# Three Gram groups take turns with two pmv groups, in place of following them

## The chip, the cores and the metric

The kernel runs on one core of one Trainium2 chip. The metric is device time in microseconds, as the median of several runs. One execution was also recorded by the hardware profiler; its rows are quoted below. TensorE (PE in the rows, its weight loads PEld), VectorE (DVE), ScalarE (ACT), GpSimd (POOL) and SyncE (SP) are the five engines.

## The reference

One inference step of a two-layer model for 512 latent and 128 context tokens of width 2048, in float32. Layer 0 holds two kinds of attention heads. Layer 1, in which the change lies, is a bidirectional RWKV-7 mixer with 32 heads of 64 channels. After projections that give r, k, v, a gate and, per direction, a decay w and a rate a, it runs this scan over the tokens, once forwards and once backwards:

```python
def step(s, inp):
    r_t, w_t, k_t, v_t, kk_t, a_t = inp
    sa = jnp.einsum('bhij,bhj->bhi', s, -kk_t)
    s = s * w_t[:, :, None, :] + sa[..., None] * (kk_t * a_t)[:, :, None, :] + v_t[..., None] * k_t[:, :, None, :]
    return s, jnp.einsum('bhij,bhj->bhi', s, r_t)
```

The two directions are normalised per head, get a bonus term (the sum over a head of r, k and a weight, times v), are added, gated and projected.

## The kernel before, in words

**Units.** Layer 1 works on 16 tiles of 128 channels (two heads h). Each tile has two units, u = 0 and u = 1, so that `seq` (line 1443) lists 32 units. A unit covers one order of the two directions z over ten chunks of 64 tokens, five per half of the tokens. Instead of stepping through tokens, a unit builds small matrices per chunk and carries the state S over five steps.

**Stages of a unit**, as far as they matter here, each a generator that yields where other work may come between:

- `stage_e` (lines 1077 to 1114) builds AR and BK, the decayed factors, on VectorE. BK has one buffer only. For each half of the tokens VectorE runs L1093, L1096, L1104, L1108 and L1109 one behind the other; L1109 is the last to write BK. AR (L1097, L1100) has two buffers.
- `stage_a2` (1116 to 1133) forms the Gram matrices GG = BK' AR, in three groups of 4, 4 and 2 chunks. A group has 16, 16 or 8 matmuls (L1126) into two PSUM banks at once, one per head; VectorE empties both with a mask (L1130).
- `stage_bk` transposes BK in three groups (L1200), and ScalarE stores the result as BKn (L1201).
- `stage_pre` (1213 ff.) first transposes v in two groups (pvt, L1220; ScalarE writes UV, L1223), then multiplies GG with UV in two pmv groups of 32 and 8 matmuls (L1236), one bank each; ScalarE stores them as MV (L1238). MV is read by the next unit's scan (L1330).
- `stage_inv` inverts small blocks in four steps. `stage_bonus` (1410 ff., only for u = 0) makes two pbn matmul pairs (L1021), each followed by a product on VectorE that writes vT (L1417).
- `stage_c` is the scan itself, five steps with three yields each.

gram, pbk, pvt, pmv, pbn and a few others all take their banks from one PSUM pool, `pg`, with two banks. A tile gets whichever bank is free first.

**The order.** TensorE's order is written out by hand (`manual_schedule`, line 1547 ff.); the planner leaves it alone and orders the other engines itself, by the order in which the code emits instructions, some of it lifted by `high_priority`. `unit(n)` (line 1483) emits first the scan of unit n with other stages at its yields, then `stage_e` of unit n + 2, and then goes through the list `P2` (line 1477): each entry takes one step of a stage, `inv`, `bk` and `pre` of unit n + 1, `a2` of unit n + 2, `bonus` of unit n, and then `fill(w)` inserts projection matmuls (L126, two per step) in proportion to the weight w. The projections of r, k, v and the gate are the bulk of TensorE's work and are spread over all units as filler; where a gate projection ends, ScalarE and VectorE work on the tile `gt` (L947, L952, L957). The weights of `P2` add up to 32.

In the old list the two pvt steps come early (`pre` in the fifth and tenth entry), the second half of the bonus in the eleventh, then both pmv groups, then the three Gram groups. The prologue before the first unit has a script of its own, which the change leaves as it is. Units 0 to 29 have both chains.

Of the kernel before, what the change touches and what calls it, by code (L numbers as in the profile page):

```python
# [53 lines left out]
def kernel(  # L54
# [785 lines left out]
    with ExitStack() as l1:  # L840
# [609 lines left out]
        def of(stage, n):  # L1450
            return stage(*seq[n]) if n < len(seq) else iter(())
# [22 lines left out]
                next(work[0], None)  # L1474

        CW = (3, 3, 2, 3)
        P2 = (('inv', 1), ('bk', 2), ('inv', 2), ('bk', 1), ('pre', 2), ('inv', 2), ('bonus', 1), ('bk', 1), ('inv', 2), ('pre', 2), ('bonus', 2), ('pre', 2), ('pre', 2), ('a2', 3), ('a2', 3), ('a2', 4))
        W2 = sum(w for _, w in P2)

        def step(g):  # L1480
            next(g, None)

        def unit(n):
# [25 lines left out]
            gens = dict(inv=inv, bk=of(stage_bk, n + 1), a2=of(stage_a2, n + 2), pre=of(stage_pre, n + 1), bonus=bonus)  # L1509
            for k, w in P2:  # L1510
                step(gens[k])
# [173 lines left out]
```

## Time and profile before

| what | us |
|---|---|
| median of 3 runs (3610.61 to 3622.48) | 3617.58 |
| the profiled execution | 3616.01 |
| its span, from the first to the last instruction | 3614.2 |
| TensorE busy in it | 3429.2 |
| VectorE busy in it | 2121.4 |

Layer 1's units lie between about 1640 and 3370 us of the span. In a row of the timeline the first number is the start in us, the second the duration, then the engine, the line, the operation, what it writes and reads, shapes and a count; in brackets stands how long the engine was idle before it and what ended that. In a row of the groups the numbers behind the bar are busy time, the mean duration of one in ns, and the idle time before them with those who ended it. In the table of windows they are length, busy time with the count, the granted clock as a share of the full one, and the share and rate of DMA.

### The profile page before, as it was taken

What the parts mean: (1) busy time and instruction counts of PE and PEld (TensorE: products, weight loads), DVE (VectorE), ACT (ScalarE), POOL (GpSimd) and SP (SyncE); (2) the same over time, 40 slices, a digit from 0 to 9 for tenths busy, and PEclk for the clock granted to TensorE, in tenths of its full rate; (3) what the DMA queues carried; (4) which work ended last, traced back from release to release, by engine and by line L of the source; (5) the groups of instructions that cost most, each with busy time, mean ns of one, the idle gap of its engine ahead of it and who ended that gap; (6) DMA issues with size and microseconds to landing.
All of it is one profiled execution on the core that took longest, in us unless ns stands there. A gap on an engine that the chain in (4) does not pass through costs nothing. (4 is left out here: it accounts for less than half of the span.)

```text
span 3614.2 us, 84002 instructions
## 1 busy us (share of the span) xinstructions
PE 3429.2 (95%) x34432; PEld 3004.6 (83%) x34432; DVE 2121.4 (59%) x4218; ACT 1564.7 (43%) x3214; POOL 1217.8 (34%) x1158
## 2 busy tenths in 40 slices
PE   8999999999999989899999999999999999999998
PEld 4788889988898888898887878788888888888898
DVE  3355655666666494536665666666676666666302
ACT  3244443444444422444544534444445445544322
POOL 1322222222232344543333333333333333333444
PEclk9999999999999999999999999999999999999999
DMA  9623433333333365332232222222222222233434
GB/s 324 228 73 99 126 100 111 109 108 108 108 105 107 114 222 166 107 97 66 70 75 60 73 63 69 72 66 68 72 71 70 72 68 72 70 77 104 153 98 143
DMA packets 388610, 376.23 MB, mean 104 GB/s; under 512 B 200512, under 2 KB 242560, under 8 KB 388224
## 3 DMA queue, kind: packets, MB, share of 16 engines
q1 hardware_dynamic: 388224, 370.86, 34.9%
q8 instruction: 270, 4.42, 0.5%
q14 instruction: 116, 0.95, 0.1%
HBM read 328.51 MB, written 42.24 MB: 103 GB/s over the span
## 5 line engine op out<-in xcount | busy, mean ns | idle before, releaser
L101 POOL TENSOR_TENSOR wlo<-raw,whi 128x512 fp32r<-128x512 f32 (+1 forms) x628 | 863.8, 1376 | 1917.9 <-PE pj L126 1207.8
L126 PE MATMUL pj<-h0hi,wlo 128*128 128x320 f32 x4448 | 1087.0, 323 | 25.3 <-POOL wlo L101 25.2
L126 PE MATMUL pj<-h0hi,whi 128*128 128x320 f32 x4448 | 1083.2, 322 | 4.3 <-ACT whi L100 3.1
L126 PE MATMUL pj<-h0lo,whi 128*128 128x320 f32 x4448 | 1077.1, 321 | 2.9 <-DVE h0lo L101 1.6
L126 PEld LDWEIGHTS pj<-h0hi,wlo 128*128 128x128 f32 x4448 | 746.2, 191 | 60.8 <-POOL wlo L101 30.0
L126 PEld LDWEIGHTS pj<-h0hi,whi 128*128 128x128 f32 x4448 | 744.3, 191 | 37.7 <-issue 7.7
L126 PEld LDWEIGHTS pj<-h0lo,whi 128*128 128x128 f32 x4448 | 747.4, 190 | 31.3 <-issue 8.0
L100 ACT ACTIVATE whi<-raw 128x512 fp32r<-128x512 f32 (+1 forms) x628 | 390.8, 623 | 752.5 <-PE pj L126 385.6
L200 DVE SCALAR_TENSOR_TENSOR aacc<-araw,scs,aacc 128x512 f32<-128x512 f32 x480 | 408.5, 900 | 17.4 <-DMA araw<-in_dram 16.3
L364 DVE TENSOR_REDUCE nm<-S 128x1 f32<-128x768 f32 (+1 forms) x120 | 98.5, 820 | 258.3 <-PE S L376 258.3
L1340 ACT ACTIVATE UV<-CC 64x128 f32<-64x128 f32 x160 | 43.2, 270 | 336.6 <-PE CC L1338 307.9
L724 DVE SCALAR_TENSOR_TENSOR x<-pj,mod,xr 128x512 f32<-128x512 f32 (+2 forms) x68 | 33.3, 526 | 250.9 <-PE pj L126 245.3
L367 ACT ACTIVATE P<-S,nm 128x768 f32<-128x768 f32 (+1 forms) x120 | 95.2, 793 | 165.7 <-DVE nm L364 165.0
L1130 DVE TENSOR_TENSOR GG<-gram,con 128x512 f32<-128x512 f32 (+1 forms) x192 | 107.5, 596 | 75.7 <-PE gram L1126 75.4
L1126 PE MATMUL gram<-AR,BK 64*128 64x128 f32 x1280 | 116.6, 296 | 19.3 <-DVE GG L1130 12.3
L1126 PEld LDWEIGHTS gram<-AR,BK 64*128 64x128 f32 x1280 | 92.5, 192 | 44.8 <-DVE GG L1130 23.3
L1062 PE MATMUL plo<-lr,lw 96*128 96x320 f32 x256 | 103.4, 486 | 9.8 <-DMA lr<-lorad 7.3
L566 PE MATMUL po<-PT,vt 128*128 128x128 f32 x800 | 103.2, 276 | 0.1
L566 PEld LDWEIGHTS po<-PT,vt 128*128 128x128 f32 x800 | 98.0, 191 | 4.2 <-issue 2.5
L1354 DVE TENSOR_TENSOR S<-CC,S 128x128 f32<-128x128 f32 (+1 forms) x112 | 29.9, 267 | 119.4 <-PE CC L1305 79.8
L1330 DVE SCALAR_TENSOR_TENSOR rhs<-CC,MV 128x128 f32<-128x128 f32 x160 | 46.2, 289 | 71.1 <-PE CC L1328 70.8
L1338 PEld LDWEIGHTS CC<-rhs,xd 64*64 64x64 f32 x1280 | 50.0, 134 | 41.9 <-DVE rhs L1330 19.5
(340 smaller groups left out, 5164.3 us busy)
## 6 DMA issues: line engine op xcount, KB each, us to landing
raw<-in_dram SPq DMA_DIRECT2D x612, 256.0 KB
araw<-in_dram SPq DMA_DIRECT2D x384, 256.0 KB
lr<-lorad SPq DMA_DIRECT2D x128, 120.0 KB
Ld<-GG SPq DMA_DIRECT2D x64, 160.0 KB
lw<-in_dram SPq DMA_DIRECT2D x128, 48.0 KB
x<-in_dram SPq DMA_DIRECT2D x16, 320.0 KB
xr<-in_dram SPq DMA_DIRECT2D x16, 320.0 KB
DD<-Xd SPq DMA_DIRECT2D x32, 160.0 KB
```

The lines of the kernel that those rows point to most:

```text
L100: act.activation(out=hi, in_=src, func=AF.Copy)
L101: (lo_eng or pool).tensor_tensor(out=lo, in0=src, in1=rf(hi), op=ALU.subtract)
L126: pe.matmul(p[:n, 0:b - a], w, x[:, kk ^ flip, a:b], start=(kk == order[0] and i == 0), stop=(kk == order[-1] + kc - 1 and i == 2))
L200: dve.scalar_tensor_tensor(out=acc[:, s], in0=raw, scalar=scs[:, k, s:s + 1], in1=acc[:, s], op0=ALU.mult, op1=ALU.add)
L364: dve.tensor_reduce(out=nm, in_=S[:, 0:nk], axis=AX.X, op=ALU.max, negate=True)
L367: act.activation(out=P[:, 0:nk], in_=S[:, 0:nk], func=AF.Exp, bias=nm, accum_out=l)
L566: pe.matmul(po[:, 0:128], H.vt[:, kt, :], PT[:, j, :], start=(j == 0), stop=(j == n - 1))
L1062: pe.matmul(ps[:, 0:HT], lw, lo, start=True, stop=True)
L1126: pe.matmul(ps[:, j * 128:(j + 1) * 128], BK[hs, c + j, :, :].rearrange("p a t -> p (a t)"), AR[hs, c + j, :, :].rearrange("p a t -> p (a ...
L1130: dve.tensor_tensor(out=GG[:, c:c + n, h, :], in0=ps[:, 0:n * 128].rearrange("p (j t) -> p j t", t=128), in1=maskg.rearrange("p (o t) -> p ...
L1330: dve.scalar_tensor_tensor(out=rhs.rearrange("p (h d) -> p h d", h=2), in0=C, scalar=-1.0, in1=un.MV[:, s, :].rearrange("p (h d) -> p h d" ...
L1338: pe.matmul(pu[z][o:o + 64, hs], xd[o:o + 64, 2 * loc[z] + h, :], rhs[o:o + 64, hs], start=True, stop=True)
```

## The change

In the second half of the list the Gram steps move between the pmv steps: pmv, pmv, Gram, Gram, Gram becomes Gram, pmv, Gram, pmv, Gram. The weight behind the first two Gram steps goes from 3 to 2 and that behind the pmv steps from 2 to 3; the last keeps 4, and the sum stays 32.

```diff
         CW = (3, 3, 2, 3)
-        P2 = (('inv', 1), ('bk', 2), ('inv', 2), ('bk', 1), ('pre', 2), ('inv', 2), ('bonus', 1), ('bk', 1), ('inv', 2), ('pre', 2), ('bonus', 2), ('pre', 2), ('pre', 2), ('a2', 3), ('a2', 3), ('a2', 4))
+        P2 = (('inv', 1), ('bk', 2), ('inv', 2), ('bk', 1), ('pre', 2), ('inv', 2), ('bonus', 1), ('bk', 1), ('inv', 2), ('pre', 2),
+              ('bonus', 2), ('a2', 2), ('pre', 3), ('a2', 2), ('pre', 3), ('a2', 4))
         W2 = sum(w for _, w in P2)
```

## The prediction

> **What bounds the kernel now.** I read first the page's head and busy times, then the groups of instructions, then the timeline of the part of a unit that the change rearranges, and last the table of windows with the granted clock.
>
> ```profile
> span 3614.2 us, 84002 instructions
> PE 3429.2 (95%) x34432; PEld 3004.6 (83%) x34432; DVE 2121.4 (59%) x4218; ACT 1564.7 (43%) x3214; POOL 1217.8 (34%) x1158
> L1126 PE MATMUL gram<-AR,BK 64*128 64x128 f32 x1280 | 116.6, 296 | 19.3 <-DVE GG L1130 12.3 <-ACT MV L1238 5.4 <-DVE BK L1109 0.4
> L1236 PE MATMUL pmv<-UV,GG 64*64 64x64 f32 x1280 | 51.1, 223 | 1.9 <-ACT MV L1238 1.6
> ```
>
> TensorE is busy for 95% of the span and its order is written out by hand, so what the change can move is the time in which TensorE stands still in front of its next instruction; the amount of its work stays. The last two rows give that time for the two chains that are to alternate: 19.3 us before the Gram matmuls and 1.9 us before the pmv matmuls, 21.2 us together. That is 0.6% of the span, and with it the ceiling for the direct gain of a better order. Of it 12.3 us is TensorE waiting for VectorE to empty Gram's PSUM banks into GG, and 7.0 us (5.4 and 1.6) for ScalarE to empty pmv's into MV.
>
> Next comes the tail of unit 6 (u = 0), from the last transpose of BK to the second Gram group.
>
> ```profile
> 2020.77 0.38 PE L1200 MATMUL pbk<-con,BK 128*128 128x128 f32 x2
> 2021.19 0.90 DVE L1093 TENSOR_TENSOR BK<-kk,az 128x320 f32<-128x320 f32 x2 [0.31 <-PE pbk L1200]
> 2022.00 1.56 DVE L1096 TENSOR_TENSOR BK<-BK,rate 128x320 f32<-128x320 f32 x2
> 2023.48 0.79 DVE L1104 TENSOR_SCALAR az<-az,vecs,ck 128x320 f32<-128x320 f32 x2
> 2024.09 0.46 PE L1021 MATMUL pbn<-hl,blkr 128*128 128x320 f32 x2
> 2024.19 0.88 DVE L1108 TENSOR_TENSOR az<-kT,az 128x320 f32<-128x320 f32 x2
> 2025.00 0.88 DVE L1109 TENSOR_TENSOR BK<-az,rate 128x320 f32<-128x320 f32 x2
> 2025.35 1.15 PE L1236 MATMUL pmv<-UV,GG 64*64 64x64 f32 x32
> 2025.80 0.48 DVE L1417 TENSOR_TENSOR vT<-vT,pbn 128x320 f32<-128x320 f32 x1
> 2027.50 0.45 PE L1236 MATMUL pmv<-UV,GG 64*64 64x64 f32 x8
> 2028.95 1.16 PE L1126 MATMUL gram<-AR,BK 64*128 64x128 f32 x16
> 2030.73 1.28 DVE L1130 TENSOR_TENSOR GG<-gram,con 128x512 f32<-128x512 f32 x2
> 2031.46 1.75 PE L1126 MATMUL gram<-AR,BK 64*128 64x128 f32 x16
> ```
>
> What is to be seen here decides the case. BK has one buffer. The next unit's BK cannot be written before the last transpose (L1200, 2020.77) has read the old one, and then VectorE needs five pairs of instructions, one behind the other (L1093, L1096, L1104, L1108, L1109), before the first half of BK is whole at 2025.00 + 0.44 = 2025.44. The first pmv group starts at 2025.35, in the same tenth of a microsecond. The first Gram group, which reads that BK, comes only at 2028.95, so today it has 3.5 us to spare. The two pmv groups and the projection matmuls behind them are its cover.
>
> **The change part by part.** *Work.* It adds and removes no instruction. Three Gram groups (16, 16 and 8 matmuls) and two pmv groups (32 and 8) stay, the sum of weights stays 32, so each unit gets as many projection steps as before. No step that issues a DMA moves: the store of GG follows the third Gram group, which keeps its place with its weight of 4. So nothing changes on SP's and POOL's queues, and the cost of the work is nothing.
>
> *The first Gram group moves to the place of the first pmv group.* It will now stand at the time at which the trace has that pmv group start; call it T. Two things must be done by then. The first half of BK (end of the first L1109) is one. The other is PSUM: the pool has two banks and a Gram group takes both at once, where a pmv group takes one. In units with u = 0 the bank used before is that of the second pbn matmuls, and it is free when the second L1417 has read it, in unit 6 at 2025.80 + 0.48 = 2026.28, that is 0.93 us after T. That a pmv group could go round this bank is seen in unit 10:
>
> ```profile
> 2247.66 1.15 PE L1236 MATMUL pmv<-UV,GG 64*64 64x64 f32 x32
> 2250.03 0.73 DVE L1109 TENSOR_TENSOR BK<-az,rate 128x320 f32<-128x320 f32 x1
> 2250.58 0.45 PE L1236 MATMUL pmv<-UV,GG 64*64 64x64 f32 x8 [0.70 <-ACT MV L1238]
> 2250.93 0.50 DVE L1109 TENSOR_TENSOR BK<-az,rate 128x320 f32<-128x320 f32 x1
> 2251.35 0.47 DVE L1417 TENSOR_TENSOR vT<-vT,pbn 128x320 f32<-128x320 f32 x1
> ```
>
> The second pmv group started at 2250.58 behind MV, before L1417 had even begun: it took the bank that the first pmv group had left. The Gram group cannot, and would stand from 2247.66 to 2251.82, 4.2 us. I read the same off the thirty units that have both chains: T from the first pmv group, and the later of the first L1109's end and, for u = 0, the second L1417's end. The first and the last of the thirty:
>
> ```profile
> 1697.84 0.88 DVE L1109 TENSOR_TENSOR BK<-az,rate 128x320 f32<-128x320 f32 x2
> 1698.19 1.15 PE L1236 MATMUL pmv<-UV,GG 64*64 64x64 f32 x32
> 1698.64 0.48 DVE L1417 TENSOR_TENSOR vT<-vT,pbn 128x320 f32<-128x320 f32 x1
> ...
> 3268.73 1.15 PE L1236 MATMUL pmv<-UV,GG 64*64 64x64 f32 x32
> L1109 DVE TENSOR_TENSOR BK<-az,rate x1: 933/933/933, 3270.2 to 3270.2; 128x320 f32<-128x320 f32 x1
> ```
>
> They give 1698.64 + 0.48 - 1698.19 = 0.93 us and 3270.21 + 0.93 - 3268.73 = 2.41 us. The fifteen units with u = 0 add up to 25.2 us, the fifteen with u = 1 to 16.3, together 41.5. One unit has none; in the quiet ones it is 0.5 to 0.9 us, the bare length of VectorE's row of instructions; where VectorE also has the gate projection's gt in between it is 1.2 to 4.2. TensorE takes its instructions in order, so the projection matmuls behind the Gram group wait too, and since TensorE is the full engine nothing gives that time back. Term: **+41.5 us**. From below, if only the bare row of instructions remained, thirty times 0.85 or 25 us; nothing only if VectorE's order changed.
>
> *The waits that go.* Behind the change each evacuation has another chain's group and five units of weight before its bank is asked for again by its own chain. The 7.0 us behind MV should go, and the wait of the second and third Gram group for GG. But the first pmv group now comes two units of weight behind the first Gram group and needs a bank of it. Two units lasted 2026.50 to 2027.50, 1.0 us; three, between Gram groups, 2030.11 to 2031.46, 1.35 us. The first of the two GG evacuations needs 0.64 us of its own, so it fits, unless VectorE is late, as it was here, 0.6 us behind the end of the group. I leave half of the 12.3 us standing (6.1), and the 0.4 us for BK, which is in the prologue. Term: 21.2 - 6.1 - 0.4 = **-14.7 us**; the bounds are 0 and -21.
>
> *The clock.* A wait costs more than its length when it halves TensorE's granted clock.
>
> ```profile
> 1918.62 2.67 PE L1126 MATMUL gram<-AR,BK 64*128 64x128 f32 x16 [2.60 <-DVE GG L1130]
> 1918.82:1925.64 6.82, 6.82 (x35) 0.50 0.27 79
> 2147.51:2150.92 3.41, 3.41 (x16) 0.50 0.45 96
> 2195.30:2198.71 3.41, 3.41 (x20) 0.50 0.23 71
> 3277.33:3284.15 6.82, 6.38 (x31) 0.50 0.64 234
> 2386.44:2389.86 3.42, 3.42 (x39) 1.00 0.29 76
> 1915.41:1918.82 3.41, 0.81 (x6) 1.00 0.11 27
> 2191.89:2195.30 3.41, 2.11 (x20) 1.00 0.00 2
> 2249.91:2253.32 3.41, 2.74 (x31) 1.00 0.35 112
> ```
>
> The columns are length, TensorE's busy time and count, clock, DMA. Four stretches at 0.50 lie in or just behind these tails, 20.46 us in all, and half of each is lost: x35 in 6.82 us against x39 in 3.42 at full clock. They follow stretches of 3.41 us in which TensorE was busy for 0.81 and 2.11 us; one with 2.74 was not followed by any. If the waits that cause them go, that is 20.46 / 2 = **-10.2 us**. The new waits bring others. Eight of the thirty are 1.8 us or longer, more than the 1.3 us that the stretch with 2.11 lacked, so I let each of the eight halve the clock for the mean of those seen, 20.46 / 4 = 5.1 us, and lose 2.6: **+20.5 us**, with bounds of 0 and, were all 29 waits to do it, 8 x 2.6 + 21 x 1.7 = 56.
>
> Here a rule speaks otherwise. The Trainium skill, "TensorE: Matmul & The Clock Gate", section "HAM oscillation — how this bites in real kernels", puts the abstract rule as "no PE-idle gaps >~3.4µs". By it only the wait of 4.2 us could halve the clock, and the sum would lack nearly all of the last term. The row with 2.11 us busy disagrees: 1.3 us of idle time was enough. I keep the trace's price and carry the rule's outcome as a rival.
>
> *Sum.* 41.5 - 14.7 - 10.2 + 20.5 = +37.1 us. The profiled execution took 3616.0 us (its span of 3614.2 and 1.8 around it), which gives 3653.1; the median of the runs, 3617.6, lies 1.6 above it, so I predict **3655 us**, 1.0% slower.
>
> **The rivals.** *No new halvings* (0.20). The waits come as forecast but are spread so that no stretch lacks enough. For it: the row with 0.7 us idle (2.74 busy) kept its clock. Against: the one with 1.3 us did not. Sum 41.5 - 14.7 - 10.2 = +16.6, 3634 us.
>
> *Only the bare row of VectorE instructions remains* (0.12). The order on VectorE is the planner's and not written out, and it may put gt's instructions behind BK's when the Gram group is next. Then 25 - 14.7 - 10.2 = 0, 3618 us: nothing to see.
>
> *The cover outlasts the move: faster* (0.10). If the planner puts L1417 and L1109 ahead of gt and of the second halves, BK and the bank are ready at T, as in the one unit without a wait. Then only the gains are left, -14.7 - 10.2 = -24.9, 3593 us. It decides from the point at which the waits at the first Gram group fall below 24.9 us in all, 0.83 a unit. Against it: after the last transpose the five pairs have VectorE to themselves in the quiet units, and still end 0.1 us (u = 0) to 0.8 us (u = 1) behind T, with L1417 behind them.
>
> *Every wait halves the clock* (0.08): 41.5 - 14.7 - 10.2 + 56 = +73, 3690 us.
>
> That the change does not do what it says is no case: the list is the order in which the kernel writes TensorE's groups, and the planner leaves that order as written.
>
> **How the numbers follow.** The forecast has 0.50; its own range, with 25 to 41.5 us of waits and 15 to 35 for the clock, is 3635 to 3675. What a measurement of this kernel can tell from no change is about 0.3%, 11 us, so up to 3628 counts as no change. Slower: forecast, first and last rival, 0.78; same 0.12; faster 0.10. The range from 3613 to 3685 leaves out the faster case and most of the last.
>
> **What would show it.** In the changed kernel the idle time before the Gram matmuls should be 35 to 45 us, most of it in front of first groups, released by BK (L1109) for u = 1 and by vT (L1417) for u = 0; that before the pmv matmuls under 8 us; idle time behind MV near zero; and eight or so stretches at half clock right behind first Gram groups between 1690 and 3290 us. If first Gram groups start at T without idle time, the forecast is wrong by its largest term; if they wait and the clock holds, by its last.

## The result, and the profile after

The changed kernel takes 3656.5 us (median of 4 runs, 3646.2 to 3659.8) against 3615.0 us for the old one (median of 4, one more than when the forecast was made): a ratio of 1.0114, 95% interval 1.0085 to 1.0142. It is slower by 41.5 us, 1.1%; 37 were forecast, over the median known then. The profiled execution took 3653.6 us. Its head, and the groups of the two chains:

```profile
span 3651.8 us, 84032 instructions
PE 3431.3 (94%) x34432; PEld 3006.2 (82%) x34432; DVE 2123.0 (58%) x4218; ACT 1572.0 (43%) x3214; POOL 1207.6 (33%) x1158
L1126 PE MATMUL gram<-AR,BK 64*128 64x128 f32 x1280 | 110.4, 296 | 36.3 <-DVE BK L1109 28.4 <-DVE vT L1417 5.0 <-ACT pj L109 1.1
L1236 PE MATMUL pmv<-UV,GG 64*64 64x64 f32 x1280 | 54.8, 233 | 22.5 <-DVE GG L1130 22.3
```

TensorE's busy time is the same to 2 us of 3430, and the span is 37.6 us longer. The idle time before the two chains rose from 19.3 + 1.9 = 21.2 us to 36.3 + 22.5 = 58.8 us, which is 37.6 us as well. That the two figures agree to the tenth is chance: the busy time grew by 2.1 us, and TensorE's other idle time fell by 2.1. Who is waited for has changed: before it was GG and MV in front of Gram, now it is BK and vT in front of Gram, and GG in front of pmv.

The same tail of unit 6 on the timeline of the changed kernel, with VectorE's rows and those of the two chains:

```profile
2032.03 0.89 DVE L1093 TENSOR_TENSOR BK<-kk,az 128x320 f32<-128x320 f32 x2 [0.31 <-PE pbk L1200]
...
2035.84 0.88 DVE L1109 TENSOR_TENSOR BK<-az,rate 128x320 f32<-128x320 f32 x2
2036.46 0.46 PE L1126 MATMUL gram<-AR,BK 64*128 64x128 f32 x2 [0.20 <-ACT gt L947]
2036.64 0.48 DVE L1417 TENSOR_TENSOR vT<-vT,pbn 128x320 f32<-128x320 f32 x1
2037.17 1.16 PE L1126 MATMUL gram<-AR,BK 64*128 64x128 f32 x14 [0.25 <-DVE vT L1417]
...
2037.50 0.80 DVE L1389 TENSOR_REDUCE gst<-ysq 128x10 f32<-128x640 f32 x1
2038.22 0.54 DVE L952 SCALAR_TENSOR_TENSOR gt<-pj,vecs,gt 128x320 f32<-128x320 f32 x1
2038.68 1.27 DVE L1130 TENSOR_TENSOR GG<-gram,con 128x512 f32<-128x512 f32 x2
2039.41 1.15 PE L1236 MATMUL pmv<-UV,GG 64*64 64x64 f32 x32
```

From L1093 to the end of the first L1109 it takes 4.3 us, as before. The Gram group starts 0.18 us behind that end, at 2036.46; the row puts its wait of 0.20 us down to ScalarE's gt (L947) and not to BK, which was ready at 2036.28. It is stopped after two of its sixteen matmuls, and goes on when L1417 has emptied the second bank. So these rows show the second half of the forecast's mechanism, the bank. The first half, the wait for BK, stands clearly in a unit with u = 1 that is shown below (3089.24, 0.89 us).

### The profile page after: what moved, and what is told of

Read it like the earlier page. It is cut to its first block, busy times and chain, and to the rows that moved or that the text cites. A ratio compares the mean times of both kernels' runs of the same rounds, so it can differ in the third digit from the quotient of the medians.

```text
span 3651.8 us, 84032 instructions
## 1 busy us (share of the span) xinstructions
PE 3431.3 (94%) x34432; PEld 3006.2 (82%) x34432; DVE 2123.0 (58%) x4218; ACT 1572.0 (43%) x3214; POOL 1207.6 (33%) x1158
## 4 chain that ended last, share of the span: by engine, by line
PE 38%; DVE 15%; DMA 4%; issue 3%; ACT 2%; POOL 2%; SPq 0%; POOLq 0%; DVEq 0%; ACTq 0%
PE pj L126 26%; PE gram L1126 2%; PE plo L1062 2%; PE pmv L1236 1%; PE CC L1338 1%; POOL wlo L101 1%; DVE BK L1096 1%; PE CC L1348 1%; DVE aacc L200 1%; DVE D L1082 1%; DVE sb L1175 1%; PE CC L1328 1%; DMA araw<-in_dram 1%; DVE BK L1093 1%; DVE az L1104 1%
## 5 line engine op out<-in xcount | busy, mean ns | idle before, releaser
L101 POOL TENSOR_TENSOR wlo<-raw,whi 128x512 fp32r<-128x512 f32 (+1 forms) x628 | 852.5, 1358 | 1969.1 <-PE pj L126 1239.2
L200 DVE SCALAR_TENSOR_TENSOR aacc<-araw,scs,aacc 128x512 f32<-128x512 f32 x480 | 408.4, 899 | 17.9 <-DMA araw<-in_dram 17.0
L1126 PE MATMUL gram<-AR,BK 64*128 64x128 f32 x1280 | 110.4, 296 | 36.3 <-DVE BK L1109 28.4
L1126 PEld LDWEIGHTS gram<-AR,BK 64*128 64x128 f32 x1280 | 89.2, 194 | 59.4 <-issue 28.8
```

The costliest lines, as they stand in the source:

```text
L101: (lo_eng or pool).tensor_tensor(out=lo, in0=src, in1=rf(hi), op=ALU.subtract)
L200: dve.scalar_tensor_tensor(out=acc[:, s], in0=raw, scalar=scs[:, k, s:s + 1], in1=acc[:, s], op0=ALU.mult, op1=ALU.add)
L1126: pe.matmul(ps[:, j * 128:(j + 1) * 128], BK[hs, c + j, :, :].rearrange("p a t -> p (a t)"), AR[hs, c + j, :, :].rearrange("p a t -> p (a ...
```

## The experiments

The theories: **A**, the first Gram group comes before BK and vT are done, and the first pmv group too close behind it; this is the forecast's own mechanism. **B**, the weights of 2 in place of 3 cost the time. **C**, two chains that take turns on two banks hinder each other. Two more came in on the way: **D**, what is late is VectorE's queue as a whole, and GG stands in it behind further work. **W**, two units of weight are too short in themselves. Waits are idle time before the matmuls of L1126 and L1236 in one profiled execution; ratios stand against the old kernel as it was run beside each of them, with 95% intervals. A profiled execution can lie off the median of its runs (e2's took 3645.7 us where the median is 3631.9, e3's 3641.5 where it is 3650.5), so the waits and the ratios of the table don't match to the us.

| run | Gram waits | pmv waits | both, us | ratio |
|---|---|---|---|---|
| old kernel | 19.3 | 1.9 | 21.2 | 1 |
| changed kernel | 36.3 | 22.5 | 58.8 | 1.0114 (1.0085 to 1.0142) |
| e1, old order, new weights | 19.7 | 1.9 | 21.6 | 1.0012 (0.9998 to 1.0026) |
| e3, new order, old weights | 36.7 | 13.9 | 50.6 | 1.0082 (1.0060 to 1.0105) |
| e2, pmv first, then by turns | 21.4 | 14.3 | 35.7 | 1.0036 (1.0020 to 1.0052) |
| e5, new order, 1.0 us later | 17.4 | 40.2 | 57.6 | 1.0115 (1.0095 to 1.0135) |
| e4b, Gram without BK | 19.6 | 43.6 | 63.2 | 1.0139 (1.0109 to 1.0170) |
| e6, new order, Gram urgent | 35.4 | 22.7 | 58.1 | 1.0098 (1.0068 to 1.0128) |
| e9, VectorE relieved | 40.8 | 2.7 | 43.5 | 1.0077 (1.0062 to 1.0092) |
| e7, old order, Gram urgent | 17.4 | 1.9 | 19.3 | 0.9980 (0.9965 to 0.9995) |
| e10, old order, weights 2 3 3 3 3 | 17.6 | 3.7 | 21.3 | 0.9976 (0.9963 to 0.9989) |
| e8, e7 and e10 together | 13.6 | 2.9 | 16.5 | 0.9955 (0.9937 to 0.9973) |
| e11, e8 with weights 2 4 3 3 2 | 12.6 | 2.7 | 15.3 | 0.9969 (0.9956 to 0.9982) |

**Weights alone.** The edit to the old list (only its end is shown, here and below):

```diff
-('bonus', 2), ('pre', 2), ('pre', 2), ('a2', 3), ('a2', 3), ('a2', 4)
+('bonus', 2), ('pre', 3), ('pre', 3), ('a2', 2), ('a2', 2), ('a2', 4)
```

> The old order (pmv, pmv, Gram, Gram, Gram) with the new weights (3, 3, 2, 2, 4). Theory A (place): the change costs time because the first Gram group comes before VectorE has finished BK and vT, and the first pmv group too close behind it. Then here no wait for BK or vT (under 2 us in all), but two units of weight, 1.0 us, are too short for two GG evacuations of 1.28 us, so 15 to 25 us more of waiting for GG before the second and third Gram group: 3625 to 3640 us. Theory B (weights): the weights of 2 in place of 3 behind Gram are what costs; then about the time of the changed kernel, 3656 us. Theory C (alternation): two chains on two banks hinder each other by taking turns; then as before, 3615 us.

Measured: 3624.4 us, 1.0012, no change clear of the noise. Theory B falls: the weights alone do next to nothing. Theory C's figure, no change, held. Theory A's was a miss: waits for GG rose from 12.3 to 15.2 us and not by 15 to 25. That the two units of weight that moved ahead of the first Gram group gave VectorE the time is likely, but no run shows it.

**Order alone.**

```diff
-('bonus', 2), ('pre', 2), ('pre', 2), ('a2', 3), ('a2', 3), ('a2', 4)
+('bonus', 2), ('a2', 3), ('pre', 2), ('a2', 3), ('pre', 2), ('a2', 4)
```

> The new order with the old weights (Gram 3, pmv 2, Gram 3, pmv 2, Gram 4). Theory A: the waits for BK and vT before the first Gram group stay (33 to 36 us), the wait of the first pmv group for GG falls from 22 to about 12 us: 3640 to 3650 us. Theory B: back to the time before, 3615 us. Theory C: as the changed kernel, 3656 us.

Measured: 3650.5 us, 1.0082, half a us above A's band. The Gram waits stay (36.7), the pmv waits fall from 22.5 to 13.9 us, as A had it. The order makes most of the loss, which B did not allow. One unit of weight more behind Gram and one less behind pmv take away 8.6 us of waiting; in the time this is not clear of the noise, as the intervals of the two kernels overlap, so C's 3656 us is not ruled out by this run.

**pmv first.**

```diff
-('bonus', 2), ('pre', 2), ('pre', 2), ('a2', 3), ('a2', 3), ('a2', 4)
+('bonus', 2), ('pre', 2), ('a2', 3), ('pre', 2), ('a2', 3), ('a2', 4)
```

> Alternation with the pmv group first: pmv, Gram, pmv, Gram, Gram with weights 2, 3, 2, 3, 4. The first Gram group comes 2.15 us later than in the changed kernel. Theory A: the waits before the first Gram group fall from 36 to 4 us (what exceeds 2.15 us in the thirty units), and those for GG under 10; no slower than before, 3600 to 3618 us. Theory B: as before, since the weights behind Gram are 3. Theory C: slower than before by 20 us or more, since the chains still take turns on two banks.

Measured: 3631.9 us, 1.0036. A was wrong on the time and on GG: the waits for BK were nearly gone (1.8 us), as it said, but those for GG were 20.9 us and not under 10, and it was slower. The groups of this run say by what:

```profile
L1126 PE MATMUL gram<-AR,BK 64*128 64x128 f32 x1280 | 112.8, 295 | 21.4 <-ACT MV L1238 11.6 <-DVE GG L1130 6.9 <-DVE BK L1109 1.8
L1236 PE MATMUL pmv<-UV,GG 64*64 64x64 f32 x1280 | 51.2, 223 | 14.3 <-DVE GG L1130 14.0 <-ACT UV L1223 0.2
```

Now 14.0 us are the second pmv group's wait for GG and 11.6 us Gram's for MV. B falls again, since the weights behind Gram were 3 and it was still slower; C's loss of 20 us or more did not come either, but something like C is there: each chain waits until the other's bank has been emptied.

**The alternation 1.0 us later.**

```diff
-('bonus', 2), ('a2', 2), ('pre', 3), ('a2', 2), ('pre', 3), ('a2', 4)
+('bonus', 4), ('a2', 2), ('pre', 3), ('a2', 2), ('pre', 3), ('a2', 2)
```

> The changed kernel with two units of weight moved from behind the last Gram group to ahead of the first one (bonus 4, last Gram 2), so that the whole alternation comes 1.0 us later. Theory A: the waits before the first Gram group fall from 36 to 16 us (what exceeds 1.0 us), the pmv wait for GG from 22 to about 15, and fewer stretches at half clock: 3622 to 3635 us. Theories B and C: weights and alternation are those of the changed kernel, so 3650 to 3660 us.

Measured: 3659.1 us, 1.0115, no better than the changed kernel, as B and C had it; B had fallen with the first run. Theory A as it stood falls here. Its figure for Gram is right (17.4 us, forecast 16), but pmv's waits went up to 40.2 us. Here is the timeline of one quiet unit (one without the gate's gt in between) with u = 1, first in the old kernel, then in the changed one, then in this run. Only rows of VectorE and of the two chains on TensorE are shown:

```profile
3058.23 1.15 PE L1236 MATMUL pmv<-UV,GG 64*64 64x64 f32 x32
3058.59 0.88 DVE L1109 TENSOR_TENSOR BK<-az,rate 128x320 f32<-128x320 f32 x2
3059.39 0.81 DVE L1389 TENSOR_REDUCE gst<-ysq 128x10 f32<-128x640 f32 x1
3060.24 1.79 DVE L1415 SCALAR_TENSOR_TENSOR kzs<-rT,vecs,kzs 128x320 f32<-128x320 f32 x2
3060.38 0.45 PE L1236 MATMUL pmv<-UV,GG 64*64 64x64 f32 x8
3061.83 1.33 PE L1126 MATMUL gram<-AR,BK 64*128 64x128 f32 x16
3061.95 1.07 DVE L1392 TENSOR_TENSOR Yn<-Yn,gst 128x640 f32<-128x640 f32 x1
3063.03 1.29 DVE L1130 TENSOR_TENSOR GG<-gram,con 128x512 f32<-128x512 f32 x2
```

```profile
3088.62 0.88 DVE L1109 TENSOR_TENSOR BK<-az,rate 128x320 f32<-128x320 f32 x2
3089.24 1.25 PE L1126 MATMUL gram<-AR,BK 64*128 64x128 f32 x16 [0.89 <-DVE BK L1109]
3089.42 0.81 DVE L1389 TENSOR_REDUCE gst<-ysq 128x10 f32<-128x640 f32 x1
3090.26 1.80 DVE L1415 SCALAR_TENSOR_TENSOR kzs<-rT,vecs,kzs 128x320 f32<-128x320 f32 x2
3091.98 1.27 DVE L1130 TENSOR_TENSOR GG<-gram,con 128x512 f32<-128x512 f32 x2
3092.71 1.15 PE L1236 MATMUL pmv<-UV,GG 64*64 64x64 f32 x32 [1.14 <-DVE GG L1130]
```

```profile
3079.30 0.88 DVE L1109 TENSOR_TENSOR BK<-az,rate 128x320 f32<-128x320 f32 x2
3079.92 1.25 PE L1126 MATMUL gram<-AR,BK 64*128 64x128 f32 x16
3080.10 0.81 DVE L1389 TENSOR_REDUCE gst<-ysq 128x10 f32<-128x640 f32 x1
3080.94 1.79 DVE L1415 SCALAR_TENSOR_TENSOR kzs<-rT,vecs,kzs 128x320 f32<-128x320 f32 x2
3082.66 1.88 DVE L1392 TENSOR_TENSOR Yn<-Yn,gst 128x640 f32<-128x640 f32 x1
3084.46 1.28 DVE L1130 TENSOR_TENSOR GG<-gram,con 128x512 f32<-128x512 f32 x2
3085.19 1.15 PE L1236 MATMUL pmv<-UV,GG 64*64 64x64 f32 x32 [2.95 <-DVE GG L1130]
```

In all three VectorE goes on behind BK with the group norm's sum (L1389) and the bonus product (L1415), 2.6 us. In the old kernel TensorE spends that time on the pmv groups and the projection matmuls behind them; Gram ends at 3061.83 + 1.33 = 3063.16, and GG has begun on its banks at 3063.03, without delay. In the changed kernel Gram is done at 3090.49 and GG starts 1.5 us later. In the run with the later alternation the planner put L1392 in between as well, and pmv waited 2.95 us. From this comes theory D: the two pmv groups covered not only BK's row but the rest of VectorE's work up to GG. The next runs test it.

**Gram without BK.** The Gram matmuls read AR on both sides and the mask is scaled by 0.01, on top of the changed kernel; the true Gram matrices are left out.

```diff
-                                  BK[hs, c + j, :, :].rearrange("p a t -> p (a t)"),
+                                  AR[hs, c + j, :, :].rearrange("p a t -> p (a t)"),
...
-    maskg = np.where(t < 64, s < t % 64, s <= t % 64)
+    maskg = 0.01 * np.where(t < 64, s < t % 64, s <= t % 64)
```

> The changed kernel, but the Gram matmuls read AR on both sides in place of BK and AR, and the mask is scaled by 0.01 to keep the values small: the Gram matrices are left out as such, all instructions stay. So the first Gram group no longer waits for BK. Theory A (BK is what is late): the 36 us before the first Gram groups fall to the 5 to 13 us of vT, the 22 us before pmv stay, and the time falls to 3625 to 3635 us. Theory D (VectorE's queue as a whole is late, and GG stands behind the same instructions in it as BK's last): the wait moves from Gram to pmv, which rises to 40 us or more, and the time stays at 3645 to 3660 us.

Measured: 3666.9 us, 1.0139. The same unit in this run, with the same choice of rows:

```profile
3090.26 1.16 PE L1126 MATMUL gram<-AR 64*128 64x128 f32 x16
3090.59 0.88 DVE L1109 TENSOR_TENSOR BK<-az,rate 128x320 f32<-128x320 f32 x2
3091.39 0.81 DVE L1389 TENSOR_REDUCE gst<-ysq 128x10 f32<-128x640 f32 x1
3092.23 1.78 DVE L1415 SCALAR_TENSOR_TENSOR kzs<-rT,vecs,kzs 128x320 f32<-128x320 f32 x2
3093.94 1.27 DVE L1130 TENSOR_TENSOR GG<-gram,con 128x512 f32<-128x512 f32 x2
3094.67 1.15 PE L1236 MATMUL pmv<-UV,GG 64*64 64x64 f32 x32 [2.18 <-DVE GG L1130]
```

Gram does not wait for BK any more; it starts before L1109. But GG comes behind L1109, L1389 and L1415 as ever, and pmv waits 2.18 us in place of 0.89 before Gram and 1.14 before pmv. Over the kernel Gram's waits fall to 19.6 us (18.6 of them vT), pmv's rise to 43.6. D had forecast the 40 us or more, A that pmv's waits stay and the time falls. The time lies above D's band too (3645 to 3660); where that comes from was not followed up.

**Gram urgent, in the new and in the old order.** On the changed kernel and on the old one:

```diff
-        gens = dict(..., a2=of(stage_a2, n + 2), ...)
+        gens = dict(..., a2=urgent(of(stage_a2, n + 2)), ...)
```

> The changed kernel with the Gram stage emitted at high priority, so that the planner puts GG on VectorE ahead of the group norm's sums (L1389, L1392), the bonus product (L1415) and gt where these are ready at the same time. Theory D: the 22 us of pmv waiting for GG fall under 8, the 36 us before Gram stay: 3635 to 3645 us. If two units of weight are too short in themselves (theory W), the pmv wait stays over 15 us and the time at 3650 to 3660 us.

> The old order with the Gram stage emitted at high priority. Theory D: the 12.3 us of Gram waiting for GG in the old kernel are VectorE's queue too and fall under 5; the time falls by 5 to 15 us, to 3602 to 3612 us. Theory W: unchanged, 3613 to 3620 us.

Measured in the new order: 3654.4 us, 1.0098, with pmv's waits as they were (22.7). D's figures were missed, and W's were met. The quiet unit shows why the run does not decide between them all the same:

```profile
3088.82 0.80 DVE L1389 TENSOR_REDUCE gst<-ysq 128x10 f32<-128x640 f32 x1
3089.65 1.79 DVE L1415 SCALAR_TENSOR_TENSOR kzs<-rT,vecs,kzs 128x320 f32<-128x320 f32 x2
3091.37 1.27 DVE L1130 TENSOR_TENSOR GG<-gram,con 128x512 f32<-128x512 f32 x2
```

L1389 and L1415 still stand ahead of GG, so the priority did not change VectorE's order there, and what D says was not put to the test. In the old order: 3610.7 us, 0.9980, inside D's band; but Gram's waits for GG fell from 12.3 to 9.3 us and not under 5, as D had it.

**VectorE relieved.** On the changed kernel the group norm's second sum is left out (the square of the mean stands for the variance) and r_k is left out of the bonus; two products go to GpSimd.

```diff
-            dve.tensor_reduce(out=var, in_=c3(ysq), axis=AX.X, op=ALU.add)
+            dve.tensor_tensor(out=var, in0=mean, in1=mean, op=ALU.mult)
...
-            dve.tensor_tensor(out=Yq, in0=Yq, in1=bc(var), op=ALU.mult)
+            pool.tensor_tensor(out=Yq, in0=Yq, in1=bc(var), op=ALU.mult)
...
-                dve.scalar_tensor_tensor(out=t.kzs[:, a:b], in0=t.rT[:, a:b], scalar=rk64[:, i:i + 1], in1=t.kzs[:, a:b],
-                                         op0=ALU.mult, op1=ALU.mult)
+                pool.tensor_tensor(out=t.kzs[:, a:b], in0=t.rT[:, a:b], in1=t.kzs[:, a:b], op=ALU.mult)
```

> The changed kernel with VectorE relieved of what the planner puts between BK and GG: the group norm's second sum (L1389) is left out (the square of the mean stands for the variance), the product with it (L1392) and the bonus product (L1415, without r_k) go to GpSimd. Theory D (GG stands on VectorE behind those instructions): the 22 us of pmv waiting for GG fall under 9, the 36 us before the first Gram groups stay within 30 to 37, and the time falls by 10 to 20 us against the changed kernel, to 3636 to 3646 us. Theory W (two units of weight are too short in themselves): the pmv wait stays over 15 us and the time at 3650 or more.

Measured: 3644.7 us, 1.0077. The groups (L1417 is line 1416 here), and the quiet unit:

```profile
L1126 PE MATMUL gram<-AR,BK 64*128 64x128 f32 x1280 | 112.1, 297 | 40.8 <-DVE BK L1109 32.0 <-DVE vT L1416 5.7 <-ACT pj L109 1.1
L1236 PE MATMUL pmv<-UV,GG 64*64 64x64 f32 x1280 | 53.9, 231 | 2.7 <-DVE GG L1130 2.5
3080.93 0.88 DVE L1109 TENSOR_TENSOR BK<-az,rate 128x320 f32<-128x320 f32 x2
3081.56 1.25 PE L1126 MATMUL gram<-AR,BK 64*128 64x128 f32 x16 [0.90 <-DVE BK L1109]
3082.72 1.29 DVE L1130 TENSOR_TENSOR GG<-gram,con 128x512 f32<-128x512 f32 x2 [0.91 <-PE gram L1126]
3083.81 1.15 PE L1236 MATMUL pmv<-UV,GG 64*64 64x64 f32 x32
```

GG follows Gram at once, and pmv's waits are gone (2.7 us) with weights and order unchanged, so W falls and D stands. C by itself falls as a cause of pmv's wait too, since the chains still take turns on the same two banks. That pmv needs a bank which GG has to empty remains a condition; a third bank was not tried. Gram's waits are a little above the band named (40.8). The two parts of the waiting are thereby shown apart: the row up to BK, and the instructions between BK and GG. In time the run is 0.37% below the changed kernel's ratio, 13 us for 15.3 us less waiting, though the ends of the two intervals overlap.

**Versions of the old order.**

```diff
-('bonus', 2), ('pre', 2), ('pre', 2), ('a2', 3), ('a2', 3), ('a2', 4)
+('bonus', 2), ('pre', 2), ('pre', 3), ('a2', 3), ('a2', 3), ('a2', 3)
```

This is e10; with Gram urgent besides it is e8. In e11 Gram is urgent and the weights are:

```diff
-('bonus', 2), ('pre', 2), ('pre', 2), ('a2', 3), ('a2', 3), ('a2', 4)
+('bonus', 2), ('pre', 2), ('pre', 4), ('a2', 3), ('a2', 3), ('a2', 2)
```

In the texts that follow, "the fastest version" is e8, and in e8's own text "the run before" is e7.

> The old order with one unit of weight moved from behind the last Gram group to behind the second pmv group (2, 3, 3, 3, 3), without the high priority of Gram. It parts the two edits of the fastest version. Of the 7.0 us of waiting for MV about 4 go, and with 1.0 us more of cover some of the 12.3 for GG: 3606 to 3614 us under theory D. If the gain came from the priority alone, 3614 to 3620.

> As the run before, and one unit of weight moved from behind the last Gram group to behind the second pmv group (pmv 2, pmv 3, Gram 3, 3, 3). Of the 7 us of waiting for MV about 5 go as well: 3598 to 3608 us under theory D; under theory W 3608 to 3616.

> The fastest version so far with one more unit of weight moved from behind the last Gram group to behind the second pmv group (2, 4, 3, 3, 2), so that the Gram groups come later still. Theory D: the waits before Gram fall from 13.6 to about 9 us; 3597 to 3605 us. If the cover before Gram is already enough, no change against that version, or a loss through the shorter stretch before the scan.

Measured: e10 3609.1 us (0.9976), e8 3603.6 (0.9955), e11 3603.3 (0.9969). All three are faster than the old kernel clear of their intervals, by 0.2 to 0.5%, and their times lie in the bands named under D. The waits do not: those for MV (Gram's and pmv's) fell from 7.0 us only to 5.6 in e10 and 4.5 in e8, where 3 and 2 were forecast, and Gram's waits in e11 are 12.6 us and not 9. So the times were hit without the stated reason. The intervals of e8 and e11 overlap, so the further unit of weight is not shown to bring or cost anything. e10's two waits add up to what the old kernel has, 21.3 us, and it is 8 us faster all the same; where that comes from stays open. Its profiled execution was at half clock for 17.1 us between 1600 and 3420 us of the span, the old kernel's for 41.0, but one execution of each does not show that this is the cause. The Gram group of e8:

```profile
L1126 PE MATMUL gram<-AR,BK 64*128 64x128 f32 x1280 | 111.5, 289 | 13.6 <-DVE GG L1130 8.1 <-ACT MV L1238 2.8 <-DVE BK L1109 0.4
```

Against the old kernel's 12.3 and 5.4 us, Gram waits less for GG and for MV, as both edits meant.

## Why the prediction was right, point by point

*The work stays:* right, 3429.2 and 3431.3 us busy with the same count.

*The first Gram group's wait, +41.5 us:* right in place, 6 us too large in size. Before the first Gram groups of the thirty units TensorE stood idle for 35.2 us: 17.3 with u = 1, where 16.3 were forecast, and 17.9 with u = 0, where 25.2 were. So the difference lies with u = 0. There the forecast let the whole group wait for the second bank; in unit 6 two of its matmuls ran for 0.46 us while the bank was late. If it is so in all fifteen units, that is 6.9 us, by estimate. The sign named for u = 0, release by vT, held only in part: the rows put 10.7 us there down to BK (L1109), 5.0 to vT (L1417) and the rest to ScalarE.

*The waits that go, -14.7 us, with 6.1 us left for pmv:* this is the step whose size was wrong. What was to go did go: no wait for MV is left before Gram or pmv that the rows name, and the second and third Gram groups wait 0.6 us for GG. But the first pmv group waits 22.3 us for GG, in 21 of the thirty units, and not 6.1. I had reckoned GG's own 0.64 us against the 1.0 us of two weights and had let VectorE be late only now and then. It is late in most units, since the planner lays the group norm and the bonus product between BK and GG; e9 shows that these are the cause. The sign named for this, waits before pmv under 8 us, failed. With it the two chains' waits rose by 37.6 us, against 41.5 - 14.7 = 26.8 forecast.

*The clock, -10.2 + 20.5 us:* right in kind, too large in size. In the windows of the changed kernel (length, busy time and count, clock, DMA):

```profile
2197.07:2200.33 3.26, 1.53 (x18) 1.00 0.29 85
2200.33:2203.75 3.42, 2.88 (x34) 0.50 0.00 0
2702.09:2705.51 3.42, 1.06 (x8) 1.00 0.19 56
2705.51:2712.33 6.82, 6.62 (x55) 0.50 0.09 34
```

As in the old kernel, a stretch of about 3.4 us in which TensorE was idle for a good part is followed by a stretch of 3.4 or 6.8 us at half clock, called a halving here. TensorE was busy for 0.46 to 1.69 us in the stretches ahead of the changed kernel's halvings, and for 0.81 to 2.21 in the old one's. There are eight halvings in or behind the tails, six of 3.4 us and two of 6.8, 34.1 us in all, against four and 20.5 us before. Six of the eight stand behind first Gram groups, in six of the eight units whose wait the forecast put at 1.8 us or more; the other two, at 2538 and 2650 us, follow waits of pmv. Half of the difference is 6.8 us, where 10.3 was forecast. But that is still too much. Between the first Gram group and the last pmv group of the span (1600 to 3331 us before, 1602 to 3370 after) the old kernel has three more halvings outside the tails and the changed one two, and TensorE was busy there for 1657.1 and 1659.8 us: that is 2.7 us more work time only. The Trainium skill's rule ("TensorE: Matmul & The Clock Gate", section "HAM oscillation — how this bites in real kernels": no idle gaps over about 3.4 us) does not hold here as the limit: the first stretch above lacked 1.7 us of work and was followed by half clock, so the measurement decides. Only one wait in the two chains, 3.5 us for BK in unit 10, was longer than the rule's figure.

*The sum:* the span grew by 37.6 us, which are 37.6 of waiting in the two chains, 2.1 of busy time and -2.1 of idle time elsewhere; nearly the whole loss is waiting. The forecast of 37.1 had 26.8 for the waits and 10.3 for the clock. The waits were 11 us too small, because of pmv, and the clock about 8 us too large, so that they nearly cancel. The direction and the main mechanism were understood; that the time came out within 2 us is luck. The range that the forecast calls its own, 3635 to 3675, does not quite follow from the bounds it gives: they make 3633 to 3669.

*The rivals:* "no new halvings" fell with the eight stretches, "the cover outlasts the move" with the 35.2 us, above its point of 24.9; "only the bare row remains" with both; "every wait halves the clock" with eight halvings out of thirty units.

## What to carry to other kernels

A group of matmuls that looks movable may be the cover for another engine's queue: before moving it, read on that engine's timeline everything between the instruction that the moved group waits for and the one that empties its banks, and not the dependency alone. If a wait is removed and the time stays, look at the next instruction behind the same queue; here leaving BK out of Gram's matmuls took 17 us of waiting from Gram and brought 21 to pmv.

## What the runs showed of the hardware that was not expected

Little. TensorE's clock was halved behind stretches that were far from empty: 1.7 us without work in a stretch of 3.3 us was enough for 3.4 us at half clock, as 1.3 us in 3.4 had been in the old kernel. It is no sharp limit: in the changed kernel TensorE was busy for only 1.67 of the 3.40 us from 1869.20 on, as far as the profile's records go, and the next 3.40 us still ran at the full clock.
